# Attention tiles of 128 keys at the ends of a sequence, with queries of dilation 4 rotated by 64

## The chip, the cores and the metric

The kernel runs on one core of a Trainium2 chip. The metric is the device time of one execution in microseconds (us); a kernel is run several times, and the median counts. One execution is also recorded by the hardware profiler: its page has the busy time of each engine (PE = TensorE matmul, PEld = TensorE weight load, DVE = VectorE, ACT = ScalarE, POOL = GpSimd, SP = SyncE, which here only issues transfers), and its trace has the start and duration of each instruction. L1364 is line 1364 of the kernel.

## The reference

One layer of a hybrid encoder is applied to a long sequence of 1024 tokens and a short one of 512, with the same weights, in f32. Branch A is a bidirectional mLSTM. Branch B, which the change touches, is dilated sliding-window attention: three groups with 8 heads of 64 each, and for a group of dilation `dil` each query sees the keys at offsets `m*dil` with |m| <= 64. The core of it:

```python
def dilated_group(q, k, v, dil, half, bias_table):
    ...
    off = np.arange(kb_len)[None, :] - half - np.arange(A_QBLOCK)[:, None]
    key_pos = idx - half
    mask = (np.abs(off) <= half)[None] & ((key_pos >= 0) & (key_pos < l_))[:, None, :]
    bias = bias_table.astype(jnp.float32)[t5_bucket(off * dil)].transpose(2, 0, 1)
    logits = jnp.einsum('bghnqe,bghnke->bghnqk', qr, kb) + bias[:, None]
    logits = jnp.where(mask, logits, -jnp.inf)
    mx = jnp.max(logits, axis=-1)
    p = jnp.exp(logits - mx[..., None])
    den = jnp.sum(p, axis=-1)
    o = jnp.einsum('bghnqk,bghnke->bghnqe', p, vb)
```

The dilations are 1, 4 and 16, and half is 64 throughout. The positions of one residue (position modulo dilation) form a sequence of their own of length `l_`; a key before its start or behind its end is masked. The three groups' outputs are mixed by their row maxima `mx` and denominators `den`.

## The kernel before

The program goes through four large parts. A first one, the pair stage, makes the projections of the long sequence, two column units at a time (38 pairs). Then come, for the long sequence, the mLSTM and the attention; and then the same two for the short one, and an end. From the mLSTM on, the order of PE and SP is the order of the code (`manual_schedule`), and a `Fill` puts projections of the short sequence, and later the output projections, between the steps: `fill.stage(steps, shares)` fixes how many fill steps fall on a round of attention. In the pair stage all engines, and later ACT, DVE and POOL, are ordered by a planner that models the times of the instructions.

**Units and tiles.** `attention` (L1306) makes the tiles of a unit; a unit `u` is one group `g` and one pair `pr` of heads, so that there are 12 units for each sequence, u = 0 to 3 of dilation 1, 4 to 7 of dilation 4, 8 to 11 of dilation 16 (which the kernel splits by 8 or by 4 residues, with the mask in the bias). A unit has S / 128 tiles of 128 queries, 8 in the long sequence and 4 in the short. It is `wide` if a residue has over 128 positions: dilation 1 in both sequences, and dilation 4 in the long one, where a residue has 256. A wide tile has 256 keys, a narrow one 128. A tile is a tuple (place of its queries, place of its keys, key blocks, bias table, rows of the output to write).

- Dilation 1: the queries are stored rotated by 64 positions, so that tile `a` holds queries 64 + 128 a to 191 + 128 a, and their keys are those of blocks a and a + 1. The last tile holds the last 64 queries of the sequence and the first 64; it takes key blocks n - 1 and 0, and a bias table `b1` of its own, which POOL makes from `b0` with a copy and two memsets to -1e30 (`ends`, L1335, kept in `self.later` and run halfway through the unit, L1459).
- Dilation 4, wide: each residue has two tiles of 128 queries, both against all 256 keys of it, with two bias tables, offsets 0 and -128 (L1342).
- Narrow: one tile per 128 positions, with its own 128 keys and one table.

**Stages of a tile** (`stages`, L1351), for two heads each: `products` puts q k into `lg` in PSUM (wide: two f32r matmuls a head; for the last tile of dilation 1, whose blocks do not adjoin, four of 128 columns a head); `softmax` adds the bias and takes the row maximum in one DVE reduction a head, negates the maxima, and lets ACT take the exponent with its row sum; `turn` transposes each block of 128 keys on PE into `pt` and copies it to SBUF (ACT for odd tiles, DVE for even); `output` multiplies by v on PE, one f32 matmul of 64 columns per head and key block, into `o`, and ACT copies that to `ot`, which SP writes to `og` in DRAM. `att_round` (L1475) does, in one round, the products and the softmax of neighbouring tiles, the transposes of a tile two rounds old, one share of the fill, and the output of a tile three rounds old.

**Loads.** While unit i runs, the loads for unit i + 1 are put into a list (`queue`, L238): for a wide unit 4 of the queries, 8 of the keys, for every second unit the values, and then the bias tables, two loads each. `spread(T.n - 1)` (L1450, L241) sets the pace to the length of the list over 7 rounds of the long sequence, rounded up, and each `tick` (L231) issues so many on SP. `need` issues what is still missing when a unit begins. There are four buffers for bias tables (`bias`), taken in turn; queries and keys have two. Writes of `og` are put on SP three ticks after they are made (`lag`), in the same queue as the loads.

**The queries.** `att_unit` (L760) takes a unit of 128 projected columns, scales the queries by 1/8 and splits them into a high and a low f32r part (ACT writes `hi`, DVE writes `lo`), sorted by residue; for dilation 1 in two parts, so that they lie rotated. It serves the pair stage (`pwk`, from `c`) and the short sequence's fill (`sw`, from `dense`).

## Time and profile before

| | us |
|---|---|
| median of 3 runs | 2254.23 (2253.35 to 2256.43) |
| profiled execution, its own time | 2252.45 |
| its span, first to last instruction | 2250.7 |
| granted TensorE clock | 0.999 of full |

The busy time of PE is modelled at the ends of its matmuls, which overlap, so that two that follow each other are better compared by their starts. In a group's row stand line, engine, operation, output and inputs, size and count, then busy time and the mean of one in ns, then the idle time of the engine just before and what ended it. In a row of waits stand who waited for whom, the total in us, how often, and the longest. In the timeline stand start and duration in us, engine, line, operation and count; neighbours of one kind are merged into one row.

### The profile page before, as it was taken

Reading aid. Unit: us, or ns where it says so; the run is one execution under the profiler, and the core shown is the slowest. Engines: PE = TensorE matmul, PEld = TensorE weight load, DVE = VectorE, ACT = ScalarE, POOL = GpSimd, SP = SyncE. Lnnn points to the kernel's source line nnn. Section 1 sums busy time; section 2 is a strip of 40 time slices with the busy share of each in tenths; the row PEclk is TensorE's granted clock in tenths of the full one; section 3 lists DMA queues with packets and bytes.
Section 4 is the critical chain, followed back from the end, with each engine's and each line's share of the span. In section 5 each row is a group of like instructions: output and inputs, shape, how many; then the busy total and the mean of one; then the engine's idle time right before and its main releaser. Section 6 shows DMA issues by size and latency. Waiting matters only on the chain.

```text
span 2250.7 us, 35392 instructions
## 1 busy us (share of the span) xinstructions
PE 2238.9 (99%) x12226; PEld 1964.4 (87%) x12226; DVE 1510.2 (67%) x2875; ACT 1128.0 (50%) x2369; POOL 713.5 (32%) x1000
## 2 busy tenths in 40 slices
PE   9999999999999999999999999999999999999998
PEld 8999888888888888888888899999888888888887
DVE  7765577687776665558887754544689854655674
ACT  6432244444443443457776655666665644554332
POOL 1000333333333222237676610011165522221221
PEclk9999999999999999999999999999999999999999
DMA  3652455543233223284664788997678897776663
GB/s 123 172 131 76 174 202 192 195 178 120 107 111 112 85 84 131 104 294 167 224 212 133 202 213 231 257 254 212 202 244 285 253 269 222 232 258 199 225 236 114
DMA packets 222685, 418.27 MB, mean 186 GB/s; under 512 B 24841, under 2 KB 128969, under 8 KB 222506
## 3 DMA queue, kind: packets, MB, share of 16 engines
q1 hardware_dynamic: 194536, 315.86, 44.3%
q0 software_dynamic: 24368, 87.56, 12.4%
q10 hardware_dynamic: 3602, 12.59, 1.4%
q8 instruction: 97, 1.59, 0.3%
q14 instruction: 82, 0.67, 0.1%
HBM read 296.19 MB, written 128.12 MB: 189 GB/s over the span
## 4 chain that ended last, share of the span: by engine, by line
PE 97%; issue 1%; DMA 1%; DVE 0%; ACT 0%; POOL 0%; DVEq 0%; POOLq 0%; ACTq 0%
PE d L211 14%; PE d L209 14%; PE d L210 14%; PE dense L209 12%; PE dense L211 12%; PE dense L210 12%; PE o L1400 4%; PE pt L1387 2%; PE lg L1364 2%; PE num L209 1%; PE num L211 1%; PE num L210 1%; PE a L1072 1%; PE kv L209 1%; PE kv L210 1%
## 5 line engine op out<-in xcount | busy, mean ns | idle before, releaser
L209 PE MATMUL dense<-H,wh 128*128 128x512 f32 x664 | 270.3, 407 | 0.0
L211 PE MATMUL dense<-H,wl 128*128 128x512 f32 x664 | 260.6, 393 | 0.0
L210 PE MATMUL dense<-H,wh 128*128 128x512 f32 x664 | 260.4, 392 | 0.0
L210 PE MATMUL d<-Hl,phla 128*128 128x512 f32 x608 | 236.5, 389 | 0.0
L211 PE MATMUL d<-Hh,phla 128*128 128x512 f32 x608 | 236.5, 389 | 0.0
L209 PE MATMUL d<-Hh,phla 128*128 128x512 f32 x608 | 236.5, 389 | 0.0
L278 DVE TENSOR_TENSOR wl<-wraw,wh 128x1024 fp32r<-128x1024 f32 (+1 forms) x121 | 149.5, 1236 | 66.4 <-ACT wh L272 66.3
L1376 DVE CUSTOM_DVE_ANT_0 ls<-lg,bias 128x256 f32<-128x256 f32 (+1 forms) x288 | 93.7, 362 | 135.2 <-PE lg L1364 69.8
L211 PE MATMUL d<-Hh,phlb 128*128 128x512 f32 x456 | 177.4, 389 | 0.0
L209 PE MATMUL d<-Hh,phlb 128*128 128x512 f32 x456 | 177.4, 389 | 0.0
L210 PE MATMUL d<-Hl,phlb 128*128 128x512 f32 x456 | 177.4, 389 | 0.0
L1380 ACT ACTIVATE ls<-ls,nm 128x256 f32<-128x256 f32 (+1 forms) x288 | 129.9, 452 | 83.3 <-DVE nm L1378 58.2
L687 POOL TENSOR_TENSOR psum_w<-pw_raw 128x512 f32<-128x512 f32 x38 | 55.0, 1447 | 366.0 <-DMA pw_raw<-w_in 222.5
L272 ACT ACTIVATE wh<-wraw 128x1024 fp32r<-128x1024 f32 (+1 forms) x124 | 128.5, 1037 | 72.4 <-PE dense L210 26.4
L211 PEld LDWEIGHTS dense<-H,wl 128*128 128x128 f32 x664 | 124.7, 188 | 28.1
L209 PE MATMUL d<-vhi,Hh 128*128 128x322 f32 x448 | 140.9, 314 | 0.3
L211 PE MATMUL d<-vhi,Hl 128*128 128x322 f32 x448 | 140.3, 313 | 0.4 <-DVE Hl L396 0.2
L210 PE MATMUL d<-vlo,Hh 128*128 128x322 f32 x448 | 139.6, 312 | 0.0
L210 PEld LDWEIGHTS dense<-H,wh 128*128 128x128 f32 x664 | 125.3, 189 | 14.3
L209 PEld LDWEIGHTS dense<-H,wh 128*128 128x128 f32 x664 | 125.0, 188 | 14.4
L209 PEld LDWEIGHTS d<-Hh,phla 128*128 128x128 f32 x608 | 114.1, 188 | 23.7
L210 PEld LDWEIGHTS d<-Hl,phla 128*128 128x128 f32 x608 | 114.1, 188 | 23.7
(570 smaller groups left out, 6158.5 us busy)
## 6 DMA issues: line engine op xcount, KB each, us to landing
pw_raw<-w_in SPq DMA_DIRECT2D x76, 512.0 KB
wraw<-w_in SPq DMA_DIRECT2D x64, 512.0 KB
aqk_a<-pwk SPq DMA_DIRECT2D x48, 512.0 KB
aqk_b<-sw SPq DMA_DIRECT2D x48, 256.0 KB
wraw<-w_pm POOLq DMA_DIRECT2D x24, 512.0 KB, 5.8
wraw<-w_out POOLq DMA_DIRECT2D x24, 512.0 KB, 3.9
wraw<-w_v POOLq DMA_DIRECT2D x22, 430.0 KB, 6.1
erep<-erow SPq DMA_DIRECT2D x16, 512.0 KB
```

The source lines that it names most:

```text
L209: nc.tensor.matmul(out, lh, rh, start=start, stop=False)
L210: nc.tensor.matmul(out, lh, rl, start=False, stop=False)
L211: nc.tensor.matmul(out, ll, rh, start=False, stop=stop)
L272: high = nc.scalar.activation(hi[:, :n], raw[:, :n], AF.Copy)
L278: low = (self.lows or nc.vector).tensor_sub(lo[:, :n], raw[:, :n], hi[:, :n].bitcast(F32))
L687: self.nc.gpsimd.tensor_add(s[:, 0], ws[1][:, 0], ws[1][:, 1])
L1072: nc.tensor.matmul(p[:, c - c0], kT[:, ct, c * P:(c + 1) * P], qT[:, ct, c * P:(c + 1) * P], start=ct == 0, stop=ct == 1)
L1364: nc.tensor.matmul(lg[:, hh, c:c + w], q[hh][:, qs], z[:, k0:k0 + w], start=z is k[hh], stop=z is not k[hh])
L1376: nc.vector.tensor_tensor_reduce(out=ls[:, hh], in0=ts["lg"][hh], in1=bt[:, hh], scale=1.0, scalar=NEG, op0=OP.add, op1=OP.max, accum_out= ...
L1380: self.held = self.held[-3:] + [nc.scalar.activation(ls[:, hh], ls[:, hh], AF.Exp, bias=nm[:, hh:hh + 1], accum_out=ot[:, 128 + hh:129 + hh])]
L1387: nc.tensor.transpose(pp[:, hh * nk + x], ts["ls"][:, hh, x * P:(x + 1) * P], self.ident)
L1400: nc.tensor.matmul(po[:, hh * 64:hh * 64 + 64], pt[:, hh * nk + x], v[:, kt[x], c0 + hh * 64:c0 + hh * 64 + 64], start=x == 0, stop=x == n ...
```

## The change

Queries of dilation 4 in the long sequence are stored rotated by 64 positions in each residue, as those of dilation 1 are. Each residue then has one tile with queries 64 to 191 against all its 256 keys, and one end tile with the last 64 queries in rows 0 to 63 (`late`) and the first 64 in rows 64 to 127 (`early`). The last tile of dilation 1 is such an end tile too, in both sequences. Late queries see only keys of the last block, early ones only keys of the first, so that an end tile keeps 128 keys a row: its products are still made with both blocks (now one matmul of 256 columns over two blocks, which may lie apart), but the softmax takes, per head, the 128 columns that live for the late rows and those for the early ones in two reductions, both with table `b0`. Exponent, transposes and the copy of `pt` work on 128 columns a head. The output multiplies by both blocks' values side by side (128 columns a head), and ACT copies from them the late and the early rows in two instructions. All wide units use one bias table; `ends` and `self.later` go.

```diff
--- before.py
+++ after.py
@@ -765,6 +765,10 @@
         hi, lo = w(F32R), w(F32R)
         if g == 0 and not keys:
             parts = [(hi[:, :S - 64], lo[:, :S - 64], c[:, 64:]), (hi[:, S - 64:], lo[:, S - 64:], c[:, :64])]
+        elif not keys and S // dil > P:
+            by = lambda z: z.rearrange("p (r i) -> p r i", r=dil)
+            x, n = c.rearrange("p (i r) -> p r i", r=dil), S // dil - 64
+            parts = [(by(hi)[:, :, :n], by(lo)[:, :, :n], x[:, :, 64:]), (by(hi)[:, :, n:], by(lo)[:, :, n:], x[:, :, :64])]
         else:
             by = lambda z: z.rearrange("p (r i) -> p r i", r=dil)
             parts = [(by(hi), by(lo), c.rearrange("p (i r) -> p r i", r=dil))]
@@ -1325,31 +1329,25 @@
 
 
         og = T.og[:, g, pr]
-        tiles, later = [], self.later
+        tiles, H = [], 64
+        early, late = slice(H, P), slice(0, H)
+        b0 = table(-H if wide else 0)
         if g == 0:
-            b0 = table(-64)
             for a in range(n - 1):
-                tiles.append((P * a, P * a, (a, a + 1), b0, [(0, P, 64 + P * a, 1)]))
-            b1 = bias().rearrange("p (h w) -> p h w", h=2)
-
-            def ends():
-                nc.gpsimd.tensor_copy(b1, b0)
-                nc.gpsimd.memset(b1[0:64, :, P:W], NEG)
-                nc.gpsimd.memset(b1[64:P, :, 0:P], NEG)
-            later[u] = ends
-            tiles.append((S - P, S - P, (n - 1, 0), b1, [(0, 64, S - 64, 1), (64, 64, 0, 1)]))
+                tiles.append((P * a, P * a, (a, a + 1), b0, [(0, P, H + P * a, 1)], False))
+            tiles.append((S - P, 0, (0, n - 1), b0, [(0, H, S - H, 1), (H, H, 0, 1)], True))
         elif wide:
-            bs = (table(0), table(-P))
             for r in range(dil):
-                for x in range(2):
-                    tiles.append((r * L + x * P, r * L, (2 * r, 2 * r + 1), bs[x], [(0, P, r + dil * P * x, dil)]))
+                tiles.append((r * L, r * L, (2 * r, 2 * r + 1), b0, [(0, P, r + dil * H, dil)], False))
+                tiles.append((r * L + P, r * L, (2 * r, 2 * r + 1), b0, [(0, H, r + dil * (L - H), dil), (H, H, r, dil)], True))
         else:
-            b0 = table(0)
             for t in range(n):
-                tiles.append((t * P, t * P, (t,), b0, [(0, P, t, dil)]))
-
-        def stages(turned, qp, kp, kt, bt, dst):
-            nk = len(kt)
+                tiles.append((t * P, t * P, (t,), b0, [(0, P, t, dil)], False))
+
+        def stages(turned, qp, kp, kt, bt, dst, ends):
+            nk = 1 if ends else len(kt)
+            W = nk * P
+            pair = slice(kt[0], kt[-1] + 1, max(kt[-1] - kt[0], 1))
             qs = slice(qp, qp + P)
             ts = {}
 
@@ -1357,12 +1355,10 @@
                 lg = self.bank("lg")
                 if wide:
                     ts["lg"] = [lg[:, 0], lg[:, 1]]
-                    runs = [(0, kp, W)] if kp + W <= S else [(0, kp, P), (P, 0, P)]
                     for hh in range(2):
-                        for c, k0, w in runs:
-                            for z in (k[hh], k[2 + hh]):
-                                nc.tensor.matmul(lg[:, hh, c:c + w], q[hh][:, qs], z[:, k0:k0 + w], start=z is k[hh],
-                                                 stop=z is not k[hh])
+                        for z in (k[hh], k[2 + hh]):
+                            nc.tensor.matmul(lg[:, hh], q[hh][:, qs], z.rearrange("p (n j) -> p n j", j=P)[:, pair],
+                                             start=z is k[hh], stop=z is not k[hh])
                 else:
                     kk = [z[:, kt[0]].rearrange("p a j -> p (a j)") for z in k]
                     ts["lg"] = [lg[:, 0, :P], lg[:, 0, P:2 * P]]
@@ -1372,9 +1368,11 @@
                 ls = ts["ls"] = sb.tile([P, 2, W], F32, name="ls", bufs=3)
                 ot = ts["ot"] = self.ot()
                 nm = sb.tile([P, 2], F32, name="nm", bufs=3)
+                blocks = [(late, slice(P, 2 * P), slice(0, P)), (early, slice(0, P), slice(P, 2 * P))]
                 for hh in range(2):
-                    nc.vector.tensor_tensor_reduce(out=ls[:, hh], in0=ts["lg"][hh], in1=bt[:, hh], scale=1.0, scalar=NEG,
-                                                   op0=OP.add, op1=OP.max, accum_out=ot[:, 130 + hh:131 + hh])
+                    for rows, of, by in blocks if ends else [(slice(0, P), slice(0, W), slice(0, W))]:
+                        nc.vector.tensor_tensor_reduce(out=ls[rows, hh], in0=ts["lg"][hh][rows, of], in1=bt[rows, hh, by], scale=1.0,
+                                                       scalar=NEG, op0=OP.add, op1=OP.max, accum_out=ot[rows, 130 + hh:131 + hh])
                 nc.vector.tensor_scalar(nm, ot[:, 130:132], -1.0, None, op0=OP.mult)
                 for hh in range(2):
                     self.held = self.held[-3:] + [nc.scalar.activation(ls[:, hh], ls[:, hh], AF.Exp, bias=nm[:, hh:hh + 1],
@@ -1395,11 +1393,20 @@
             def output():
                 pt, ot = ts["pt"], ts["ot"]
                 po = self.bank("o").rearrange("p a b -> p (a b)")
-                for hh in range(2):
-                    for x in range(nk):
-                        nc.tensor.matmul(po[:, hh * 64:hh * 64 + 64], pt[:, hh * nk + x],
-                                         v[:, kt[x], c0 + hh * 64:c0 + hh * 64 + 64], start=x == 0, stop=x == nk - 1)
-                self.held = self.held[-3:] + [nc.scalar.activation(ot[:, :128], po[:, :128], AF.Copy)]
+                vh = lambda x, hh: v[:, x, c0 + hh * 64:c0 + hh * 64 + 64]
+                if ends:
+                    for hh in range(2):
+                        nc.tensor.matmul(po[:, hh * P:hh * P + P], pt[:, hh], vh(pair, hh), start=True, stop=True)
+                    by = po[:, :2 * P].rearrange("p (h x e) -> p h x e", h=2, x=2)
+                    for x, rows in enumerate((early, late)):
+                        last = nc.scalar.activation(ot[rows, :128].rearrange("p (h e) -> p h e", h=2), by[rows, :, x], AF.Copy)
+                else:
+                    for hh in range(2):
+                        for x in range(nk):
+                            nc.tensor.matmul(po[:, hh * 64:hh * 64 + 64], pt[:, hh * nk + x], vh(kt[x], hh), start=x == 0,
+                                             stop=x == nk - 1)
+                    last = nc.scalar.activation(ot[:, :128], po[:, :128], AF.Copy)
+                self.held = self.held[-3:] + [last]
                 for p0, cnt, row, stp in dst:
                     self.put(("og", S), og[row:row + (cnt - 1) * stp + 1:stp], ot[p0:p0 + cnt], ot)
 
@@ -1438,7 +1445,6 @@
                     self.xo_bufs.insert(0, ("stage", b[2:]))
                 return self.attention(T, u, first if u == 0 else self.att_load(T, u), bias, sb, ps)
 
-            self.later = {}
             coming = ready(0)
             self.need(("table", 0))
             for i in range(12):
@@ -1456,9 +1462,6 @@
                         self.need(("att", i))
                     if j == 1:
                         self.need(("table", i))
-                    if j == T.n // 2:
-                        with self.tc.issue_after(self.loaded.ins):
-                            self.later.pop(i, lambda: None)()
                     tiles.append(t)
                     self.att_round(tiles, fill)
                     if len(tiles) in at:
```

## The prediction

> **What bounds the kernel now.** I read the page first: its span, the busy times and the chain that ended last.
>
> ```profile
> span 2250.7 us, 35392 instructions
> PE 2238.9 (99%) x12226; PEld 1964.4 (87%) x12226; DVE 1510.2 (67%) x2875; ACT 1128.0 (50%) x2369; POOL 713.5 (32%) x1000
> PE 97%; issue 1%; DMA 1%; DVE 0%; ACT 0%; POOL 0%; DVEq 0%; POOLq 0%; ACTq 0%
> ```
>
> PE is occupied for 99% of the span, and the chain is PE for 97% of it. A busy PE may still be one that is held up, so I asked next for the waits of PE alone; the answer has eight rows, longest first, of which these are the first two and the last.
>
> ```profile
> PE d L1805 <- DMA Hh<-prew: 2.4, 1, 2.4
> PE d L391 <- DVE u2b L389: 0.7, 1, 0.7
> ...
> PE d L211 <- DVE Hl L434: 0.2, 1, 0.2
> ```
>
> Five rows lie between 0.7 and 0.2 us, so all eight make at most 2.4 + 0.7 + 5 x 0.7 + 0.2 = 6.8 us of 2250.7, and none of them is for `lg`, `pt` or `o`. What sets the end is how fast PE issues. A duration is then the wrong price for a matmul, as neighbours overlap; I price by the distance from the first start of one group to the first start of the next in the timeline of PE. One round of a 256-key tile of dilation 4:
>
> ```profile
> 1436.90 1.00 PE L1400 MATMUL o<-K,pts 128*128 128x64 f32 x8
> 1437.71 0.36 PE L1364 MATMUL lg<-V0a,Q 128*128 128x256 f32 x1
> ...
> 1438.27 0.60 PE L1387 MATMUL pt<-ident,ls 128*128 128x128 f32 x4
> 1438.62 0.44 PE L209 MATMUL dense<-wh,H 128*128 128x430 f32 x1
> ```
>
> `o` holds PE for 0.81 us, `lg` (four matmuls of 256) for 0.56, `pt` (four transposes) for 0.35. A round in which the last tile of dilation 1 makes its products, here one of the short sequence, has eight matmuls of 128 instead:
>
> ```profile
> 1865.90 1.00 PE L1400 MATMUL o<-X,pts 128*128 128x64 f32 x8
> 1866.71 1.09 PE L1364 MATMUL lg<-V1a,Q 128*128 128x128 f32 x8
> 1867.64 0.62 PE L1387 MATMUL pt<-ident,ls 128*128 128x128 f32 x4
> 1868.02 0.48 PE L209 MATMUL dense<-V0b,wh 128*128 128x512 f32 x1
> ```
>
> There `lg` takes 0.93 us, and the transposes behind it 0.38. The whole stage of dilation 4 of the long sequence, from the first products of its unit 4 to those of unit 8, by the windows (length, busy PE, PEld, DVE, ACT, POOL with counts, clock, DMA share, GB/s):
>
> ```profile
> 1421.00:1530.00 109.00, 109.00 (x776) 106.80 (x776) 51.64 (x201) 68.98 (x216) 11.45 (x16) 1.00 0.93 236
> ```
>
> PE is never idle in it, and its 32 rounds take 3.41 us each.
>
> **The parts that PE sees.** Twenty-four tiles become end tiles: in the long sequence one in each of 4 units of dilation 1 and four in each of 4 units of dilation 4 (4 + 16), in the short one one in each of 4 units of dilation 1 (its units of dilation 4 have 128 keys already). The trace has tiles of 128 keys, in the narrow units:
>
> ```profile
> 1549.44 0.56 PE L1400 MATMUL o<-K,pts 128*128 128x64 f32 x4
> 1549.81 0.36 PE L209 MATMUL lg<-V0a,Q 128*128 128x256 f32 x1
> ...
> 1550.25 0.38 PE L1387 MATMUL pt<-ident,ls 128*128 128x128 f32 x2
> 1550.38 0.44 PE L209 MATMUL dense<-X,H 128*128 128x426 f32 x1
> ```
>
> *Transposes.* Two cost 0.13 us. The end tile of dilation 4 saves 0.35 - 0.13 = 0.22; that of dilation 1 takes 0.25, from 0.38.
>
> *Output.* Each f32 matmul shows as two records. Four matmuls of 64 columns (eight records, 0.81 us) become two of 128 columns (four records) whose moving operand is two blocks of 64. That form isn't in the trace. The lower bound is four records of 64 columns, 0.37 us above. The nearest row with 128 columns is
>
> ```profile
> 1202.57 1.95 PE L1072 MATMUL a<-Q,K 128*128 128x128 f32 x16
> 1204.27 0.47 PE L209 MATMUL dense<-H,wh 128*128 128x512 f32 x1
> ```
>
> 1.70 / 16 = 0.106 us a record, so 0.42 for four. The upper bound is 0.81, no gain, if the two blocks are issued apart. I take 0.42, since type, size and records are alike: 0.39 saved per tile.
>
> *Products.* The last tile of dilation 1 goes from eight matmuls of 128 to four of 256 over two blocks that lie apart: 0.93 to 0.56, 0.37 saved, and 0 if the blocks are issued apart. In dilation 4 the products stay as they are.
>
> Sum: 16 x (0.22 + 0.39) = 9.8, and 8 x (0.37 + 0.25 + 0.39) = 8.1, together **17.9 us**.
>
> [...]
>
> **The parts beside PE.** *Softmax.* Instead of two reductions of 128 rows by 256 keys there are four of 64 rows by 128.
>
> ```profile
> 1545.59 0.29 DVE L1376 CUSTOM_DVE_ANT_0 ls<-lg,bias 128x128 f32<-128x128 f32 x1 [1.94 <-ACT ot L1402]
> ...
> 1545.81 0.29 DVE L1376 CUSTOM_DVE_ANT_0 ls<-lg,bias 128x128 f32<-128x128 f32 x1
> ```
>
> One of 128 by 128 takes 0.22 us; with half the rows it lies between 0.11 and 0.22. I take 0.22, as nothing shows that rows count: at most 0.88 us a tile. Even were all of it new, sixteen tiles add 14 us to the DVE time of this stage, 51.64 of 109; the exponents need it a round ahead of the transposes, which come two rounds (about 7 us) after the products. ACT halves two exponents and the copy of `pt`, and the copy of `o` becomes two of 64 rows:
>
> ```profile
> L1380 ACT ACTIVATE ls<-ls,nm 128x256 f32<-128x256 f32 x128 | 63.9, 500 | 36.8 <-DVE nm L1378 25.4 <-issue 11.0 <-DMA og_a<-ot 0.2
> L1402 ACT ACTIVATE ot<-o 128x128 f32<-128x128 f32 x61 | 16.5, 270 | 13.0 <-PE o L1400 12.7
> ```
>
> The second copy costs 0 to 0.27, less than the 0.5 that half of two exponents of 0.50 may give, so ACT is no busier. Cost on the path 0; without that cover 24 x 0.27 = 6.5 us. Gone from POOL are a copy and two memsets per unit of dilation 1; PE never waited on them: 0.
>
> *The rotated queries.* Four units (long sequence, dilation 4) scale and split in two parts, 192 and 64 positions of each residue, which adds one ACT and one DVE instruction each. The nearest are the 64-wide ones of dilation 1, the minimum of this row:
>
> ```profile
> L772 ACT ACTIVATE pwk<-c x28: 237/2037/2224, 251.0 to 473.2; 128x1024 fp32r<-128x1024 f32 x20, 128x64 fp32r<-128x64 f32 x4, 128x960 fp32r<-128x960 f32 x4
> ```
>
> Four times 0.24 on ACT, and the like on DVE: 1.9 us, under the matmuls of the pair stage. On the path 0, at most 1.9.
>
> *Transfers.* A unit of dilation 4 loads one bias table instead of two, so 8 loads fewer, and writes 12 parts of `og` instead of 8, 16 writes more of half the size. With the medians on SP (rows below) that is 16 x 0.46 - 8 x 0.43 = 4 us more of issue, spread over a stage of 109. An end write is queued behind nothing new: its two parts wait for the same copies, and the loads behind it on SP wait with it, as now.
>
> ```profile
> L225 SPq DMA_DIRECT2D og_a<-ot x100: 319/464/2481, 1324.3 to 1629.2; - x100
> L250 SPq DMA_DIRECT2D bias<-erep x56: 319/430/1148, 1310.5 to 2049.0; - x56
> ```
>
> What does move is the pace of loads. Lines 1450 and 242 hand out ceil(queued / 7) loads a round. Without a value load a unit of dilation 4 queued 12 + 4 = 16, three a round; now 14, two a round, so that the last of 12 query and key loads leaves in the sixth round instead of the fourth. This meets units 5 and 7. Unit 3, of dilation 1, queues 14 already. Last key load of units 3 and 5 on SP, and their first products on PE:
>
> ```profile
> 1384.73 0.59 SPq L250 DMA_DIRECT2D V1b<-aqk_a  x1
> ...
> 1434.89 0.66 SPq L250 DMA_DIRECT2D V1b<-aqk_a  x1
> ```
>
> ```profile
> 1393.24 0.36 PE L1364 MATMUL lg<-V1a,Q 128*128 128x256 f32 x1
> ...
> 1447.84 0.36 PE L1364 MATMUL lg<-V1a,Q 128*128 128x256 f32 x1
> ```
>
> Unit 3 lives with 8.5 us, unit 5 has 13.0 now. Two rounds of 3.41 us and 0.6 of a shortened one leave it 13.0 - 6.8 - 0.6 = 5.6. SP's own landings are not shown; the longest median of POOL's of this size is
>
> ```profile
> ymr<-ym_a POOLq DMA_DIRECT2D x16, 256.0 KB, 5.6
> ```
>
> so that the load would land just in time. With the spread of landings I allow a wait of 0.4 for each of two units, **0.8 us** (0 to 5.3, the first rival).
>
> Forecast: 17.9 - 0.8 = 17.1 us. The profiled execution took 2252.45 us by its own clock (1.75 us outside the span); it comes to 2235.4. The runs have a median of 2254.23, 1.8 above it, so I predict **2237** on their scale, 2234 to 2240 for this case alone.
>
> **The rivals.** *The stage of dilation 4 runs into its transfers.* DMA is busy 0.93 x 109 = 101.4 us. Eight tables of 128 KB less (1.05 MB of 25.7) leave 97.2; PE wants the stage in 109 - 9.8 = 99.2. If the share can't rise over 0.93, the stage takes 97.2 / 0.93 = 104.5 and gives back 5.3 us: 2254.2 - 17.9 + 5.3 = **2242**. For it: the pace above. Against: PE waits for no transfer there now, and a table less a unit frees a buffer earlier.
>
> *Only the transposes gain.* If matmuls cost by columns streamed, or a moving operand of two blocks is issued as two, then `o` (256 columns before and after) and `lg` (1024) save nothing: 16 x 0.22 + 8 x 0.25 = 5.5 us, **2249**. Against: `lg` of eight by 128 takes 0.93 and four by 256 0.56, the same columns, and `o` with 64 costs as much a record as `a` with 128. [...]
>
> *Slower: the pair stage is planned anew.* Up to the short sequence's fill, the order of all engines comes from the planner's model, and two more instructions in four units may move the rest. PE hardly waits there now, so it can only lose. With 38 pairs of units (12 + 12 + 10 + 4 in the loops), a hold-up of 0.7 us in each makes 26.6: 2237 + 26.6 = **2264**; over (17.1 + 4.5) / 38 = 0.57 us a pair it turns slower. Against: ACT and DVE have slack, and the edit touches 4 of 38.
>
> **How the numbers follow.** Forecast 0.66, transfers 0.20, transposes only 0.08, slower 0.06. Range 2233 (0.37 for `o`, no wait) to 2246 (halfway from the transfers to the third case), leaving out little more than the last two. Within 0.2%, 4.5 us, a measurement can't tell a change: 2249.7 to 2258.7. Faster 0.90, most of the third case with it; same 0.04; slower 0.06.
>
> **What would show it.** In the profile after: `o` of end tiles as four records of 128 columns over 0.42 us, and `lg` of the last tile of dilation 1 as four of 256 over 0.56; PE's waits still under 7 us with none on `lg`; the stage of dilation 4 near 100 us instead of 109. I am wrong if `lg` waits for V1a or V1b at units 5 and 7, if `o` takes 0.8, or if the first 1310 us grow.

## The result and the profile after

| | before, us | after, us | ratio |
|---|---|---|---|
| median of 6 runs each, taken in turn | 2253.36 (2252.81 to 2256.43) | 2241.86 (2237.88 to 2247.75) | 0.9949, interval 0.9938 to 0.9960 |
| profiled execution, its own time | 2252.45 | 2237.88 | |

The kernel became faster by 11.5 us in the median, and by 14.6 in the two profiled executions, of which the one after is the fastest of its runs. Its runs also lie further apart than before: over 9.9 us instead of 3.6. So there are two things to explain: the gain, and what falls short of it in most runs but not in this one.

The page of the profile after, its span, busy times and the chain that ended last:

```profile
span 2236.1 us, 35149 instructions
...
PE 2222.0 (99%) x12050; PEld 1945.2 (87%) x12050; DVE 1517.3 (68%) x2975; ACT 1125.7 (50%) x2397; POOL 706.6 (32%) x976
...
PE 93%; DMA 3%; DVE 1%; issue 1%; ACT 1%; POOL 0%; DVEq 0%; POOLq 0%; SPq 0%; ACTq 0%
```

PE has 176 instructions fewer (16 end tiles x 6 and 8 x 10) and is 16.9 us less busy, DVE has 100 more. PE still sets the end, but 7% of the chain is now something else, where it was 3%. The waits of PE of the kernel after, longest first:

```profile
PE d L1808 <- DMA Hh<-prew: 2.3, 1, 2.3
PE d L391 <- DVE u2b L389: 0.8, 1, 0.8
PE o L1406 <- DVE pts L1390: 0.7, 1, 0.7
PE d L209 <- ACT phla L668: 0.5, 1, 0.5
PE d L211 <- DVE phla L669: 0.5, 1, 0.5
```

The first two were there before. The three that follow are new: an `o` that waits for its transposed probabilities, and two waits of `d` for `phla`, in the pair stage. Seven more rows, of 0.2 to 0.5 us, bring all waits together to about 7 us. None is for `lg`.

To see where the time went I divided both spans at the first products of the long sequence's units 0, 4 and 8 and of the short sequence's units 0 and 4. The columns are the stretch, its length, busy PE, PEld, DVE, ACT, POOL with counts, granted clock, DMA share and GB/s. Before:

```profile
0.00:1312.47 1312.47, 1308.29 (x6848) 1136.73 (x6848) 926.00 (x1323) 625.56 (x1019) 471.85 (x569) 1.00 0.45 153
1312.47:1421.03 108.56, 108.56 (x761) 104.98 (x758) 57.88 (x201) 64.86 (x197) 12.10 (x25) 1.00 0.94 250
1421.03:1529.81 108.78, 108.78 (x776) 106.58 (x775) 51.56 (x200) 68.76 (x215) 11.26 (x16) 1.00 0.93 236
1529.81:1828.48 298.67, 297.82 (x1739) 263.12 (x1738) 222.94 (x583) 189.56 (x502) 116.98 (x201) 1.00 0.77 243
1828.48:1921.82 93.34, 93.34 (x533) 81.55 (x531) 45.69 (x117) 44.28 (x109) 24.38 (x50) 1.00 0.82 242
1921.82:2250.70 328.88, 322.15 (x1583) 271.42 (x1582) 206.18 (x454) 134.98 (x330) 76.94 (x142) 0.99 0.64 211
```

And after:

```profile
0.00:1316.11 1316.11, 1310.20 (x6848) 1136.84 (x6848) 924.79 (x1327) 625.76 (x1023) 474.56 (x569) 1.00 0.45 153
1316.11:1421.08 104.97, 104.97 (x726) 101.39 (x725) 58.26 (x216) 63.71 (x198) 7.20 (x13) 1.00 0.97 257
1421.08:1520.58 99.50, 98.76 (x683) 96.29 (x682) 59.44 (x267) 65.24 (x228) 11.00 (x16) 1.00 0.96 248
1520.58:1817.28 296.70, 296.45 (x1730) 262.06 (x1728) 221.96 (x582) 190.34 (x507) 117.68 (x201) 1.00 0.78 246
1817.28:1907.79 90.51, 90.13 (x499) 77.93 (x497) 47.32 (x133) 44.30 (x113) 19.64 (x38) 1.00 0.87 248
1907.79:2236.10 328.31, 321.49 (x1577) 270.69 (x1576) 205.48 (x454) 136.34 (x331) 76.52 (x142) 1.00 0.64 211
```

The three stages with end tiles are shorter by 3.59, 9.28 and 2.83 us, the two stretches behind them by 1.97 and 0.57, and the stretch up to the first products, with as many PE instructions as before, is longer by 3.64. Together that is 3.59 + 9.28 + 2.83 + 1.97 + 0.57 - 3.64 = 14.6.

What a single end tile costs now can be read from PE's timeline of the kernel after, by the distances between starts:

```profile
1364.65 0.36 PE L1360 MATMUL lg<-V1a,Q 128*128 128x256 f32 x1
...
1365.20 0.60 PE L1385 MATMUL pt<-ident,ls 128*128 128x128 f32 x4
...
1454.31 0.60 PE L1399 MATMUL o<-K,pts 128*128 128x128 f32 x4
1454.67 0.36 PE L1360 MATMUL lg<-V1a,Q 128*128 128x256 f32 x1
...
1455.23 0.38 PE L1385 MATMUL pt<-ident,ls 128*128 128x128 f32 x2
1455.36 0.44 PE L209 MATMUL dense<-X,H 128*128 128x430 f32 x1
```

The lower four rows are dilation 4: `o` holds PE for 1454.67 - 1454.31 = 0.36 us (0.81 before), the products for 0.56, as ever, the two transposes for 0.13 (0.35 before). The upper two are the products of the last tile of dilation 1: 1365.20 - 1364.65 = 0.55, against 0.93 before.

The marks are starts of products; the transposes of a tile come two rounds after its products and the output three, so that a stage shows the saving of the tiles that fall inside. In dilation 1 these are 4 products, 3 pairs of transposes and 3 outputs: 4 x 0.37 + 3 x (0.25 + 0.45) = 3.58 us against 3.59 measured. In dilation 4 they are one pair of transposes of dilation 1, 15 of dilation 4, and 15 outputs: 0.25 + 15 x 0.22 + 15 x 0.45 = 10.3, so that the stage would take 108.78 - 10.3 = 98.5; it took 99.50. In all, 16 x 0.67 + 8 x 1.07 = 19.3 us is what PE was given back. The median shows 11.5 of them. The experiments look for the other 7.8. In the profiled execution itself the start, 3.64 us longer, is the largest part of what is missing.

### The profile page after: what moved, and what is told of

Its sections match the earlier page's. It is cut to its first block, busy times and chain, and to the rows that moved or that the text cites. A ratio compares the mean times of both kernels' runs of the same rounds, so it can differ in the third digit from the quotient of the medians.

```text
span 2236.1 us, 35149 instructions
## 1 busy us (share of the span) xinstructions
PE 2222.0 (99%) x12050; PEld 1945.2 (87%) x12050; DVE 1517.3 (68%) x2975; ACT 1125.7 (50%) x2397; POOL 706.6 (32%) x976
## 4 chain that ended last, share of the span: by engine, by line
PE 93%; DMA 3%; DVE 1%; issue 1%; ACT 1%; POOL 0%; DVEq 0%; POOLq 0%; SPq 0%; ACTq 0%
PE d L211 13%; PE d L210 13%; PE d L209 13%; PE dense L209 12%; PE dense L211 12%; PE dense L210 12%; PE o L1406 3%; PE pt L1385 2%; PE lg L1360 2%; PE num L209 1%; PE num L211 1%; PE num L210 1%; DMA vs_a<-vz 1%; PE a L1076 1%; PE kv L209 1%
## 5 line engine op out<-in xcount | busy, mean ns | idle before, releaser
L1374 DVE CUSTOM_DVE_ANT_0 ls<-lg,bias 128x256 f32<-128x256 f32 (+2 forms) x336 | 103.1, 333 | 117.8 <-PE lg L1360 53.5
L687 POOL TENSOR_TENSOR psum_w<-pw_raw 128x512 f32<-128x512 f32 x38 | 59.5, 1565 | 367.1 <-DMA pw_raw<-w_in 205.6
L1378 ACT ACTIVATE ls<-ls,nm 128x128 f32<-128x128 f32 (+1 forms) x288 | 125.3, 437 | 93.8 <-DVE nm L1376 61.4
L211 PEld LDWEIGHTS d<-Hh,phla 128*128 128x128 f32 x608 | 114.1, 188 | 24.8 <-DVE phla L669 1.2
L209 PEld LDWEIGHTS d<-Hh,phla 128*128 128x128 f32 x608 | 114.1, 188 | 24.5 <-ACT phla L668 1.0
```

Of the source, the lines that this page charges most:

```text
L209: nc.tensor.matmul(out, lh, rh, start=start, stop=False)
L211: nc.tensor.matmul(out, ll, rh, start=False, stop=stop)
L687: self.nc.gpsimd.tensor_add(s[:, 0], ws[1][:, 0], ws[1][:, 1])
L1374: nc.vector.tensor_tensor_reduce(out=ls[rows, hh], in0=ts["lg"][hh][rows, of], in1=bt[rows, hh, by], scale=1.0, scalar=NEG, op0=OP.add, op ...
L1378: self.held = self.held[-3:] + [nc.scalar.activation(ls[:, hh], ls[:, hh], AF.Exp, bias=nm[:, hh:hh + 1], accum_out=ot[:, 128 + hh:129 + hh])]
```

## The experiments

Four explanations were tried; the letters are those used below. **A**: the split of the rotated queries holds up the pair stage. **S**: the stage of dilation 4, now shorter, runs into its transfers. **T**: within S, it is the bias tables that come late, as they stand at the end of the list of loads. **L**: the loads of activation tables that another part of the fill (the `lanes`) puts on ACT, 1.28 us each in the trace of the kernel after, hold up the softmax. The first expectations, of e0, e1, e2 and e4, use two letters of their own: B is late loads in the stage of dilation 4, which later became S and T, and C is a scatter of the chip's own. Each kernel was timed beside the kernel before. They form three groups, each on a chip of its own: e0, e1, e2 and e4; the f kernels; the g kernels with e3. The kernel before took 2254.31, 2254.01 and 2253.82 us on them, so that the chips agree on it, but the changed kernel itself ran only beside the first group. Differences within a group are therefore safer than those across groups. Two marks are used throughout: the length of the start (up to the first products) and of the stage of dilation 4 in the profiled execution.

| kernel | median (lowest to highest), us | runs | ratio, 95% | start | dilation 4 |
|---|---|---|---|---|---|
| before, profiled | | | | 1312.47 | 108.78 |
| after | 2241.86 (2237.88 to 2247.75) | 6 | 0.9949, 0.9938 to 0.9960 | 1316.11 | 99.50 |
| e0_again | 2242.20 (2238.26 to 2246.51) | 5 | 0.9949, 0.9936 to 0.9963 | 1316.27 | 101.22 |
| e1_big_first | 2240.03 (2235.25 to 2242.46) | 5 | 0.9938, 0.9925 to 0.9950 | 1314.45 | 104.70 |
| e2_no_rotation | 2238.49 (2237.74 to 2242.32) | 5 | 0.9935, 0.9921 to 0.9948 | 1315.38 | 100.64 |
| e4_pace3 | 2242.04 (2237.92 to 2245.27) | 5 | 0.9943, 0.9931 to 0.9956 | 1318.50 | 105.41 |
| f1_big_tables | 2248.05 (2240.45 to 2248.84) | 5 | 0.9966, 0.9954 to 0.9978 | 1314.55 | 108.21 |
| f2_tables | 2248.58 (2240.28 to 2251.16) | 11 | 0.9972, 0.9964 to 0.9981 | 1318.85 | 107.04 |
| f3_lanes_late | 2246.13 (2242.54 to 2247.49) | 5 | 0.9961, 0.9948 to 0.9974 | 1316.43 | 106.96 |
| f4_two_tables | 2244.33 (2241.18 to 2249.75) | 6 | 0.9961, 0.9950 to 0.9972 | 1316.57 | 104.69 |
| g1_keys_again | 2236.69 (2235.32 to 2237.03) | 5 | 0.9924, 0.9910 to 0.9937 | 1315.51 | 99.51 |
| g2_loads_early | 2241.14 (2239.85 to 2242.84) | 5 | 0.9945, 0.9933 to 0.9958 | 1314.55 | 102.05 |
| g3_only_dil1 | 2248.69 (2243.75 to 2252.49) | 11 | 0.9976, 0.9967 to 0.9985 | 1316.30 | 108.31 |
| e3_split_only | 2256.42 (2253.72 to 2262.74) | 11 | 1.0014, 1.0005 to 1.0022 | 1317.07 | 108.78 |

### The changed kernel again

> The changed kernel once more, unedited, for a second profile and more times (so far 2237.9 to 2247.8 us, median 2241.9). Theory A (the small parts of the rotated queries stand on ACT in front of other work and wait for the write of the buffer that they fill; how long varies from run to run): a time of 2242 or more goes with the first products of the attention at 1317 us or later (1316.1 in the first profile, 1312.5 before), and with longer waits of the copies of the queries on ACT. Theory B (loads of the stage of dilation 4): it goes with a stage of dilation 4 longer than 99.5 us and waits of lg, the first products staying at 1316. Theory C (the scatter is the chip's): it lies in neither.

The median came again, 2242.20, and with it the width of 8 us. Its stage of dilation 4 took 101.22 where the first profile had 99.50, from the same instructions: that stage is one place where executions differ. The two totals, 2237.88 and 2238.26 us, differ by less than that, so that something else made up for it.

### The split of the rotated queries alone, in the kernel before

```diff
+        elif not keys and S // dil > P:
+            by = lambda z: z.rearrange("p (r i) -> p r i", r=dil)
+            x = c.rearrange("p (i r) -> p r i", r=dil)
+            parts = [(by(hi)[:, :, 64:], by(lo)[:, :, 64:], x[:, :, 64:]), (by(hi)[:, :, :64], by(lo)[:, :, :64], x[:, :, :64])]
```

> The kernel before, with the queries of dilation 4 scaled and split in two parts (192 and 64 positions) but not rotated; attention as before the change. A: ACT waits for the writes of aqk as in the changed kernel, PE loses 1.6 to 2.2 us to it, 2255.5 to 2257. If the two parts cost nothing: 2254.

Two instructions more in each of four units, and nothing else, cost 2.6 us in the median (2256.42 against 2253.82; the interval of the ratio excludes 1). Where it happens is seen in the waits of ACT between 235 and 480 us, where `pwk`, the buffer of the scaled queries, waits for the write that empties it. In the kernel before, after, and with the split alone:

```profile
ACT pwk L772 <- DMA aqk_a<-pwk: 7.1, 1, 7.1
```

```profile
ACT pwk L776 <- DMA aqk_a<-pwk: 26.9, 3, 9.8
```

```profile
ACT pwk L776 <- DMA aqk_a<-pwk: 27.6, 3, 10.1
```

One such wait became three of up to 10 us. ACT's timeline shows which instruction waits, and what stands behind it; the kernel after:

```profile
320.80 0.66 ACT L776 ACTIVATE pwk<-c 128x256 fp32r<-128x256 f32 x1 [9.67 <-DMA aqk_a<-pwk]
321.36 1.04 ACT L668 ACTIVATE phla<-psum_w 128x1024 fp32r<-128x1024 f32 x1
```

and PE's timeline of the same kernel at that moment:

```profile
321.54 0.39 PE L211 MATMUL d<-Hh,phla 128*128 128x512 f32 x1
...
322.46 0.50 PE L209 MATMUL d<-Hh,phla 128*128 128x512 f32 x1 [0.54 <-ACT phla L668]
...
323.72 0.50 PE L211 MATMUL d<-Hh,phla 128*128 128x512 f32 x1 [0.53 <-DVE phla L669]
```

The waiting instruction is the small part, 128 x 256: the first 64 positions of each residue lie in the first quarter of `c`, so the planner could place it on ACT before the rest of `c` was there. It did: DVE writes the last piece of `c` only at 326.04 us, and the large part stands on ACT at 326.75. On ACT's queue it then stood for 9.67 us for a buffer, in which ACT did nothing else, and behind it the split of `phla`, which starts at 321.36 and for which PE waits. The instruction was ready early by its data and late by its buffer, and `phla` was late with it. This is theory A.

### The large part first

```diff
+        big = None
...
-            nc.scalar.activation(h, x, AF.Copy, scale=1.0 if keys else 0.125)
+            with ExitStack() as st:
+                if big is not None:
+                    st.enter_context(self.tc.issue_after(big.ins))
+                big = nc.scalar.activation(h, x, AF.Copy, scale=1.0 if keys else 0.125)
```

> The small part of the rotated queries is put behind the large one on ACT. A: ACT no longer waits for the writes, first products at 1312.5 to 1314, time 2237 to 2239 with a scatter under 4 us as before the change. B: as the changed kernel, 2242, scatter 10. C: 2242 with a scatter of 10.

The long waits for the write are gone from ACT between 235 and 480 us, the start is 1.7 us shorter than in the kernel after, and the median 2.2 us lower than that of the unchanged kernel beside it (the intervals overlap). That is less than A expected: 2240.03 instead of 2237 to 2239, a start of 1314.45 just above 1314, and a scatter of 7.2 us instead of under 4. To see how much of the start is A and how much is not, I paired PE's instructions of each trace with those of the kernel before in their order, and took the median shift of those that started in a window of 50 us; worked out from the timelines of PE:

| kernel | 0 to 50 | 100 to 150 | 250 to 300 | 300 to 350 | 1100 to 1150 | 1150 to 1200 | last (from 1300) |
|---|---|---|---|---|---|---|---|
| after | 0.80 | 1.09 | 1.09 | 2.88 | 2.89 | 2.89 | 3.64 |
| e3_split_only | -0.10 | 0.41 | 0.35 | 2.33 | 3.76 | 3.76 | 4.60 |
| e1_big_first | 0.80 | 1.36 | 1.36 | 1.36 | 1.35 | 1.35 | 1.98 |
| e2_no_rotation | 0.81 | 1.51 | 1.51 | 1.51 | 1.50 | 2.21 | 2.91 |
| g3_only_dil1 | 0.72 | 2.58 | 2.52 | 2.52 | 2.72 | 3.56 | 3.84 |

Near 320 us the two kernels with the small part first lose 1.8 and 2.0 us, and no other does. The profiles that are not in the table say the same: the four others with the small part first (e0, e4, f2, f4) lose 2.7, 2.2, 4.1 and 1.7 us there, the four others with the large part first (f1, f3, g1, g2) nothing. That is A's price, about 2 us; f2's is the largest, and in f2 the clock was at about half behind the waits (last section). The remaining shift of 2 to 4 us comes in steps of 0.3 to 1.9 at a few places, the first within 50 us, also in kernels without the split. One profile of the kernel before, 2252.45 us, is all there is to compare with, so this part may be scatter as much as cost; it stays open.

With A gone, this profiled execution (2242.01) was still no faster, since its stage of dilation 4 took 104.70 us. DVE's timeline of this kernel in that stage:

```profile
1474.89 0.42 DVE L1378 CUSTOM_DVE_ANT_0 ls<-lg,bias 128x256 f32<-128x256 f32 x1 [2.50 <-DMA bias<-erep]
...
1477.03 0.42 DVE L1378 CUSTOM_DVE_ANT_0 ls<-lg,bias 128x256 f32<-128x256 f32 x1 [1.70 <-DMA bias<-erep]
...
1477.38 0.69 DVE L1394 COPY pts<-pt 128x512 f32<-128x512 f32 x1
```

and PE's:

```profile
1470.92 1.08 PE L1410 MATMUL o<-K,pts 128*128 128x64 f32 x8 [1.22 <-DVE pts L1394]
...
1478.21 1.08 PE L1410 MATMUL o<-K,pts 128*128 128x64 f32 x8 [1.16 <-DVE nm L1380]
```

The two reductions of unit 6's first tile wait for their bias tables, DVE with them, and PE's next `o` 1.16 us for DVE. The other wait of `o`, at 1470.92, has no bias table behind it; theory L is about that one. It is in the first profile of the changed kernel too, with 0.74 us at 1470.54.

### The queries left unrotated

```diff
-        elif not keys and S // dil > P:
+        elif False:
```

The queries of dilation 4 are stored as before, without the split; everything behind is as in the changed kernel, so that this group's output is computed from other queries.

> The queries of dilation 4 are scaled and split in one part, as before, and stay where they were, so that the tiles of dilation 4 meet other queries than they should; the attention does the same work as in the changed kernel. A: as the big part first or better, first products at 1312.5, 2237 to 2239. B: 2242, since the loads are the same. C: 2242 with a scatter of 10.

2238.49, 3.7 us under the unchanged kernel beside it and 1.5 under e1. With e3 and e1 this puts the price of the split at 2 to 4 us; of the three, only e3's interval excludes that it cost nothing. The start, 1315.38, did not return to the 1312.5 that A expected. The stage of dilation 4 took 100.64 us.

### More loads a round

```diff
+                            if T.n > 4 and 4 <= i + 1 < 8:
+                                self.pace = max(self.pace, 3)
```

> Loads for units of dilation 4 again three a round. B: 2237 to 2238, the stage of dilation 4 below 99 us. A and C: as the changed kernel within 2 us, 2240 to 2244, the stage at 99.5.

The pace of three loads a round, which the prediction saw lost, was given back, and nothing came of it: 2242.04, where B expected 2237 to 2238. Its profiled execution, the slowest of its five, had the longest stage of dilation 4 of the kernels with the same loads, 105.41, with waits of `lg` for keys:

```profile
PE lg L1360 <- DMA V1a<-aqk_a: 1.2, 1, 1.2
...
PE lg L1360 <- DMA V1b<-aqk_a: 0.8, 1, 0.8
```

So loads come late there, but not because they are issued late. About 1.7 us of this stage is a clock that was at 0.52 and 0.91 behind these two waits (last section).

### The tables first, with and without the large part first

```diff
+                            if T.n > 4:
+                                self.queued.sort(key=lambda x: x[0][0] != "table")
```

> Large part first on ACT, and the bias tables of the next unit at the head of its list of loads instead of at the end (long sequence). Theory T (reductions on DVE wait for tables that land late, and the copies of pt behind them hold up PE): no wait of ls for bias; the stage of dilation 4 at 98.5 to 100 us, against 99.5 to 105.4 in the profiles of the changed kernel and its variants; 2236 to 2238. Theory S (all transfers of the stage are late, tables only among them): the waits move to key loads or value loads, stage 100 to 104, 2239 to 2241 as with the big part first alone.

> The changed kernel with the tables at the head of the list and nothing else. T: 2 us above the run that also puts the big part first, 2238 to 2240. S: 2241 to 2243, as the changed kernel.

Both came out above what either theory expected (2236 to 2241 for f1, 2238 to 2243 for f2). Against e1 and the changed kernel, which ran on another chip, they are 8.0 and 6.7 us slower; against f4 below, the changed kernel with 8 loads more and in the same group, f2 is 4.2 us slower. Theory T falls: the wait for the tables is gone, but what was put behind them, the keys, is late instead. PE's timeline of f1_big_tables, in unit 7:

```profile
1499.56 0.43 PE L1364 MATMUL lg<-V1a,Q 128*128 128x256 f32 x1 [3.26 <-DMA V1a<-aqk_a]
...
1501.21 0.58 PE L1364 MATMUL lg<-V1b,Q 128*128 128x256 f32 x1 [1.23 <-DMA V1b<-aqk_a]
...
1503.52 0.56 PE L209 MATMUL dense<-wh,H 128*128 128x430 f32 x1
1503.88 0.56 PE L210 MATMUL dense<-wl,H 128*128 128x430 f32 x1
...
1507.26 0.36 PE L209 MATMUL dense<-X,H 128*128 128x430 f32 x1
1507.45 0.36 PE L210 MATMUL dense<-X,H 128*128 128x430 f32 x1
```

The products wait 3.26 + 1.23 = 4.5 us, and the matmuls behind them are slower too: two neighbours start 0.36 us apart, where four microseconds later it is 0.19. The last section comes back to this.

### The lanes later

f1 with the fill's lanes in other rounds:

```diff
-                             lanes, range(44, 96, 10))
+                             lanes, range(66, 96, 5))
```

> As big part and tables first, and the six steps of the gates of the short sequence, which stand at tiles 44 to 94, at tiles 66 to 91, behind the stage of dilation 4. Theory L (their table loads on ACT of 1.28 us and their chain on DVE hold up the copies of pt near 1470 us): the wait of o for pts at 1470 us goes, the stage loses 1 us more (97.5 to 99), 2235 to 2237. T and S without L: no change against the run without it, within 1 us.

The `o` that waited 1.22 us in e1, and 0.72 in f1, starts without a wait:

```profile
1470.58 1.00 PE L1410 MATMUL o<-K,pts 128*128 128x64 f32 x8
```

So L is right about that wait. But the kernel took 2246.13, where L expected 2235 to 2237, and its stage 106.96. That is 1.9 us under f1 in the median, with overlapping intervals; waits for loads (2.7 us for V1a and 1.6 for V1b) are the larger part of what the stage loses.

### A second table a unit again

```diff
+        if wide and g == 1:
+            table(-P)
```

> The changed kernel, with the second table of each unit of dilation 4 loaded as before the change, though nobody reads it: 8 loads of 128 KB more in the stage. S: the stage grows by 3 to 4 us and the time to 2245 to 2246. T: the tables come one place later still, or the loads three a round again, 2241 to 2244. If transfers don't matter: 2242.

Eight loads more in the stage, which nobody reads: 2244.33, 2.5 us over the changed kernel, though on another chip and with overlapping intervals. The edit also brings back three loads a round. The direction is that of S, but this run alone doesn't show it.

### Units 6 and 7 with the keys of 4 and 5

On e1, so that it is e1 that it stands against:

```diff
-            kk = [x.rearrange("p (h s) -> p h s", h=2) for x in keys()]
+            again = S != BLK and u in (6, 7)
+            kk = self.kept_keys[u - 2] if again else [x.rearrange("p (h s) -> p h s", h=2) for x in keys()]
+            self.kept_keys = {**getattr(self, "kept_keys", {}), u: kk}
...
-                for to in (A, B):
+                for to in () if again else (A, B):
```

Units 6 and 7 compute with the keys of two other units, and load none.

> Large part first on ACT, and units 6 and 7 of the long sequence load no keys but use those of units 4 and 5: 16 loads of 256 KB, 4.2 MB of about 25, leave the stage of dilation 4, and the work of PE, DVE and ACT stays. Theory S (the stage is short of transfers since PE became faster): no wait of lg for keys, the stage at 98.3 to 99.5 us, 2235 to 2237, scatter under 5. If the waits come from the order on DVE or ACT (theory L) or of the tables (T): stage 101 to 105, 2239 to 2241 as with the big part first alone.

This is the run that speaks clearest. The median is 2236.69, 3.3 us under e1, and the five runs lie within 1.7 us instead of 7.2. The intervals of the two overlap, and e1 ran on another chip; but g2 below, e1 with all its loads, ran in the same group, and its five runs (2239.85 to 2242.84) all lie above these five (2235.32 to 2237.03). The stage of dilation 4 of e1, of e4, and of this kernel, by the windows:

```profile
1419.42:1524.12 104.70, 100.37 (x683) 96.15 (x682) 58.87 (x265) 65.28 (x228) 10.98 (x16) 1.00 0.93 236
```

```profile
1423.47:1528.88 105.41, 101.28 (x684) 97.81 (x683) 58.23 (x264) 65.32 (x228) 11.05 (x16) 0.98 0.95 231
```

```profile
1420.48:1519.99 99.51, 98.78 (x684) 96.31 (x683) 59.68 (x265) 65.83 (x228) 10.99 (x16) 1.00 0.79 205
```

With the DMA share down from 0.93 or 0.95 to 0.79, PE gets through as many instructions in 99.51 us, with one wait of 0.7, which is L's `o` again. The time, the stage and the scatter are those that S expected. The transfers are what the stage runs into; S holds.

A high DMA share alone doesn't make a stage late, though. The stage of dilation 1 has a share of 0.97 to 1.00 in the profiles of all twelve kernels with end tiles there, and took 104.97 us in nine of them and at most 0.21 more in the other three (f1, f2, f3).

### Loads earlier

On e1, the list of loads begun a round earlier and spread over eight rounds:

```diff
-                    if j == 1:
+                    if j == (0 if T.n > 4 and 0 < i < 11 else 1):
...
-                            self.spread(T.n - 1 if i or T.n > 4 else 1)
+                            self.spread(T.n - (j > 0) if i or T.n > 4 else 1)
```

> Large part first on ACT, and the loads of the next unit begin with round 0 instead of round 1 and are spread over 8 rounds (long sequence, from unit 1 on). S: a load that came 1 to 4 us late has 3.4 us more, the stage at 99 to 101, 2236 to 2238. If the queues are full all the time, starting earlier gains nothing: 2239 to 2241.

2241.14 against 2240.03 of e1: no gain, where S had expected 2236 to 2238. As with e4, when the loads are issued is not what makes them late.

### End tiles in dilation 1 alone

```diff
-        elif not keys and S // dil > P:
+        elif False:
...
-                tiles.append((r * L, r * L, (2 * r, 2 * r + 1), b0, [(0, P, r + dil * H, dil)], False))
-                tiles.append((r * L + P, r * L, (2 * r, 2 * r + 1), b0, [(0, H, r + dil * (L - H), dil), (H, H, r, dil)], True))
+                for x in range(2):
+                    tiles.append((r * L + x * P, r * L, (2 * r, 2 * r + 1), bs[x], [(0, P, r + dil * P * x, dil)], False))
```

> Only the end tiles of dilation 1, in both sequences; dilation 4 and its queries as before the change. By the starts of the groups 8 x (0.37 + 0.25 + 0.45) = 8.6 us are gained: 2245 to 2246.5, first products at 1312.5 to 1315, the stage of dilation 4 at 108.5, no wait in it, scatter like before (4 us).

8 x 1.07 = 8.6 us were to come, and 5.1 did (2248.69 against 2253.82). The stage of dilation 1 gained its 3.58 in full (104.97 instead of 108.56). The profiled execution, the slowest of the eleven, lost 3.83 in the start, which has neither split nor end tiles, and its stage of dilation 1 of the short sequence gave 1.1 us instead of 3.58; so it gained nothing. What makes executions of this kernel differ by 9 us there isn't explained by A or S, and stays open.

## Why the prediction came out as it did

2237 us was forecast, within 2233 to 2246; it became 2241.86.

**The matmuls: right, one term too small.** The transposes and the products cost what the rows of the tiles of 128 keys said. `o` was taken at 0.42 us and its lower bound given as 0.37; it took 0.36. A record with 128 columns cost no more than one with 64 (0.36 / 4 = 0.09 us against 0.81 / 8 = 0.101), and the row of `a`, the nearest, was the wrong one to choose. With 0.36 the sum is 19.3 instead of 17.9. The second rival, a gain of the transposes alone, is refuted by the same rows: neither `o` nor the products of two blocks that lie apart were issued as two.

**The rotated queries: wrong at nothing, and even at the most.** "On the path 0, at most 1.9" counted the added instructions and put them under the matmuls of the pair stage. Their size was read from a row of 64 columns, 0.24 us; the small part has 64 positions of four residues, so 256 columns, and took 0.66. Their duration is hidden all the same: in e1, which has both instructions too, PE lost nothing near 320 us. Their place in the queue is not: the small part waited up to 10 us on ACT with `phla` behind it, and PE lost 1.8 us near 320 us. The split alone cost 2.6. The first 1310 us grew by 3.6, which the prediction had named as a sign that it is wrong. What the step left out is the question which the other steps did ask, namely what is queued behind an instruction that waits. This is the mechanism of the third rival, a pair stage planned anew; its price of 0.7 us for each of 38 pairs was off by an order of size, since only four units were touched, as the prediction itself held against it.

**The waits of loads: right place, wrong reason, too small.** The term of 0.8 us (0 to 5.3) came from a pace of two loads a round instead of three. e4 and g2 take that reason away. The size depends on the execution: against 98.5 us, the stage of the five profiled executions with the same tiles and loads (after, e0, e1, e4, g2) took 99.50, 101.22, 104.70, 105.41 and 102.05, so 1.0 to 6.9 us more, 4.1 in the mean. About 1.0 of that is left in g1 too, L's wait of 0.7 in it, so that some 3 are for the transfers. The first rival had said 104.5 for the stage and 2242 for the kernel, and that is where the median is, in part by luck, since some 2 us of the shortfall are the split's, of which it knew nothing. Its arithmetic, a DMA share that can't rise over 0.93, was too simple: the kernel after reached 0.96 and 99.50 in the same execution. What the runs show is that some loads of this stage land 0.8 to 3.3 us late (e1, e4, f1), differently from execution to execution, and that this ceased with 16 key loads fewer, at a share of 0.79.

**The softmax: no cost on the path, though dearer than assumed.** The timeline of DVE, kernel after, two of the four reductions of an end tile:

```profile
1449.85 0.29 DVE L1374 CUSTOM_DVE_ANT_0 ls<-lg,bias 64x128 f32<-64x128 f32 x1
...
1450.16 0.28 DVE L1374 CUSTOM_DVE_ANT_0 ls<-lg,bias 64x128 f32<-64x128 f32 x1
```

They start 0.31 us apart, four of them 1.24 us a tile instead of the 0.88 assumed; the 0.22 that the prediction took as the upper bound was no bound. DVE's busy time in the stage of dilation 4 rose from 51.56 to 59.44 of 99.50, so that the cover held. With waits for tables in the same chain, though, as in e1, DVE is where they reach PE (1.16 us of `o` there).

**The balance.** 19.3 us given back by PE, some 2 taken by the split and some 4 in the mean lost in the stage of dilation 4, some 3 of them to its transfers, leave 13; measured were 11.5 to 12. The rest, 1 to 2 us, may lie in the small shifts of the start and in the short sequence, whose stage of dilation 1 gave 2.83 of 3.58 us in the profiled execution and 3.5 in seven others; no run isolates it. The forecast was right in sign and within its range, and too good by the two costs that it had put at 0 and at 0.8: a gain of 17.1 us was forecast, and 11.5 came. The range held because the rivals had widened it upwards, not because these costs were foreseen. Its lower end, 2233, is 2 us below what its own terms give (2254.2 - 17.9 - 24 x 0.05 = 2235.1).

**What was gained beyond it.** e1_big_first, the changed kernel with an order of two instructions fixed by hand, is the fastest version that computes the reference: 2240.03 us, 0.9938 of the kernel before. Against the changed kernel it is 2.2 us lower, which the intervals don't separate.

## What to carry to other kernels

Price a matmul edit on an engine that is never idle by the distances between starts and count the records; that sum held here to a hundredth of a microsecond in the stage where nothing waited (3.58 against 3.59). Then go through the instructions that seem free and ask of each what it may have to wait for and what is queued behind it, above all where a planner may place it early. And where a stage moves data nearly all the time, as the one of dilation 4 did with a share of 0.93, a shorter stage may meet its own transfers. The share alone doesn't tell, as the stage of dilation 1 shows: take loads out and look at the spread between runs, not at one profile, which may be the lucky one.

## What the runs showed of the hardware

**A low clock behind waits.** After the waits of 3.26 and 1.23 us in f1_big_tables, the granted clock was low; the windows of that kernel (columns as above, the clock being the last but two):

```profile
1499.00:1502.00 3.00, 1.21 (x4) 0.98 (x5) 0.17 (x1) 0.00 (x0) 0.00 (x0) 0.63 1.06 322
1502.00:1505.00 3.00, 3.00 (x12) 2.84 (x11) 1.38 (x6) 1.24 (x4) 0.00 (x0) 0.50 0.79 314
1505.00:1508.00 3.00, 3.00 (x17) 2.95 (x16) 1.26 (x9) 1.19 (x5) 0.00 (x0) 0.73 0.76 214
1508.00:1512.00 4.00, 4.00 (x29) 3.92 (x28) 1.55 (x7) 1.52 (x6) 0.00 (x0) 1.00 1.20 251
```

From 1502 to 1508 PE was busy throughout but ran at 0.50 and 0.73 of its clock, 0.50 x 3 + 0.27 x 3 = 2.3 us lost on top of the 4.5 waited.

The clock was low behind shorter waits too. In e4 they are the two for V1a and V1b, 1.21 us up to 1502.09 and 0.82 up to 1503.29:

```profile
1503.00:1506.00 3.00, 2.71 (x10) 2.63 (x11) 1.56 (x9) 1.25 (x7) 0.00 (x0) 0.52 0.94 286
1506.00:1509.00 3.00, 3.00 (x20) 2.93 (x19) 1.21 (x10) 2.24 (x8) 0.00 (x0) 0.91 0.83 196
```

That is 0.48 x 3 + 0.09 x 3 = 1.7 us of clock. In f2, whose profiled execution has the lowest granted clock of all (0.997), waits of 1.26 and 0.53 us for `phla`, near 323 us, came before a clock of about half from 324.9 to 328.3, some 1.7 of the 4.1 us that A costs there. Behind single waits of 1.2 us in e0 and e1 no such drop shows: the clock of e1's stage was 1.00 in the mean, that of e0's whole execution 0.999, as in the kernel before. So in e4 two waits of about a microsecond, close together, were followed by a loss nearly as large again; what exactly sets the clock back these runs don't show. A low clock is part of why both kernels with the tables first lost so much: their stage of dilation 4 has a mean clock of 0.97.

**Half the rows cost no less here.** The reduction of 64 rows by 128 took 0.29 us, as did that of 128 rows by 128 in the kernel before. By the distance of starts it is even dearer, 0.31 against 0.22 us (1545.59 and 1545.81 in the rows that the prediction shows). On DVE an end tile of two halves pays for both: four starts of 0.31 us, 1.24 us a tile.
